# Hybrid GLA and mixture-of-experts layer on one core: routing and collection of expert 0's rows in two steps, its down weights rounded behind the sort

## The chip, the core and the metric

The kernel runs on one core of a Trainium2 chip. The metric is the device time of one execution in microseconds. The engines are TensorE (PE, with its weight loads PEld), VectorE (DVE), ScalarE (ACT), GpSimd (POOL) and SyncE (SP), which issues most of the transfers to the DMA engines.

## The reference

One layer over 512 tokens of width 1024: a gated linear attention mixer, then a grouped top-2 mixture of 16 experts of inner width 512, then a norm. What matters here is the second half:

```python
x = x + g1 * y                                     # y: the mixer's output projection
h2 = _modulate(_rmsnorm(x, norm2_g[i]), sh2, sc2).reshape(n_lat, D_MODEL)
f = _moe(h2, w_router, b_router, w_gate_e[i], w_up_e[i], w_down_e[i])
x = x + g2 * f.reshape(bsz, t, D_MODEL)

def _moe(h, w_router, b_router, w1, w3, w2):
    scores = jax.nn.sigmoid((h @ w_router).astype(jnp.float32))
    sel = scores + b_router.astype(jnp.float32)
    grp = sel.reshape(n, N_EXPERT_GROUPS, EXPERTS_PER_GROUP)
    grp_score = jnp.sum(lax.top_k(grp, TOP_K)[0], axis=-1)
    best = jnp.argmax(grp_score, axis=-1)
    ...
    for e in range(N_EXPERTS):
        he = jax.nn.silu(h @ w1[e]) * (h @ w3[e])
        out = out + gates[:, e:e + 1] * (he @ w2[e])
```

Each token goes to two experts of one group of four. The kernel computes an expert only on the rows that are routed to it.

## The kernel before

**Tiles.** The 512 tokens are four tiles of 128 rows. Products in float32 are made of three matmuls of a faster format: each operand is split into a rounded part (a cast on ScalarE, line 56 or 281) and the rest (a subtraction on VectorE, line 57 or 282). For a chunk of weights this is `conv`; the names `wh`, `wl` and `fx` in the rows are its buffers. One chunk of 128 x 1024 costs one cast and one subtraction.

**Up to the routing.** `project` multiplies a tile by the output weights (lines 51 to 53), `second` makes the tile's second half of the new x (multiply line 717, add line 718, sum of squares on ScalarE line 719), which stays in `srg`. `turn` transposes x on TensorE (725) and copies it out of PSUM (727), `logits` multiplies it by the router weights (732), `score` transposes the result (854) and `add_bias` scales it by the norm (857). The norm itself is `ln_exp` (one VectorE operation at 824, logarithm and exponential on ScalarE at 825 and 826) and `refine` (three VectorE operations, 830 to 832). `scaled` (839) and `normed` (842, with the store to `h2d` in memory at 843) make the normalised and modulated rows, from which the later experts gather.

**Routing.** The sigmoid (904 to 907) gives `sel`. Sixteen VectorE operations (924 to 941) find the best group and its two experts and write the one-hot `ohs` for all four tiles at once; meanwhile `warm` (912) lets TensorE run 11 and later 2 matmuls whose results nobody reads. Eight matmuls of `ohs` with a triangle and with ones (943 to 947) give every token's position in its expert's list and every expert's count; `zm` (951) is the position, masked.

**Experts 0 and 1** are static: their weights are loaded early. Expert 0's rows aren't gathered but collected: `hot` (956) is the one-hot of its positions times the norm, and 32 float32 matmuls (964) of x with it give the collected, transposed rows, which ScalarE modulates (967). Its up projection takes 16 matmuls on unsplit float32 weights (1181; in the trace each float32 matmul of 964 and 1181 leaves two records), its gate product is at 1147 and 1148 (`he`), transposes at 1154, and the down projection uses `conv` on the chunks held in `su2` and `su3`.

**The other experts.** `index_of` makes the list of rows of an expert: a one-hot `ohx` (991), matmuls (997) and two small operations (999, 1018), after which GpSimd gathers the rows from `h2d` (1102). For experts 0 and 1 it is called first. Experts 2 to 15 are sorted by their counts in nine small VectorE operations (1042 to 1052), whose result `eid` gives the number of the expert. SyncE reads these numbers into registers (1305) and issues loads of 1 MB from the addresses that they give (688). Such loads go into buffers of the list `free` as these come free, with at most three outstanding. The first two go into the two halves of `srg`, tiles 0 and 1 and tiles 2 and 3, once nobody needs x there any more:

```python
free = su[4:9] + su[1:4] + [None, None, B[1], su[0]] + [srgf[:, 0:2048], srgf[:, 2048:4096]]
```

**Order.** Up to the collection each engine's instructions are issued in the order in which the code is written. Behind it a scheduler orders them by readiness and priority; `tc.issue_after(x)` puts what stands under it behind the instruction x. On each engine the order is then fixed in the program. Before, `index_of` for the static experts stands behind the last collecting matmul and the sort behind `hot`:

```python
with tc.issue_after(collected[1][1].ins):
    last, rest = index_of(0, tiles[0:NS], lambda e: zm[:, :, e], vals, two=True)
...
for n in (2, 3):
    with tc.issue_after(eidl.ins):
        scaled(n, V, 0, 1)
        normed(n)
```

Of the kernel before, what the change touches and what calls it, by code (L numbers as in the profile page):

```python
# [13 lines left out]
AF = mybir.ActivationFunctionType  # L14
OP = mybir.AluOpType
# [3 lines left out]
P = 128  # L19
# [13 lines left out]
def dit_kernel(ctx: ExitStack, tc: tile.TileContext, I, out):  # L33
# [865 lines left out]
    S.copy(lgT[:, 384:512], plg3)  # L899
    refine(3)  # L900
    score(3)
    for n in range(4):
# [20 lines left out]
    f_, e_ = sg4.unsqueeze(2).to_broadcast([P, 16, 4, 4]), sg4.unsqueeze(3).to_broadcast([P, 16, 4, 4])
    V.tensor_tensor(mx, pr[:, :, 0], pr[:, :, 1], op=OP.max)
    V.tensor_tensor(mn, pr[:, :, 0], pr[:, :, 1], op=OP.add)
    V.tensor_tensor(cb, f_, e_, op=OP.is_equal)
    V.tensor_add(m1, mx[:, :, 0], mx[:, :, 1])
    V.tensor_tensor(m2_, mn[:, :, 0], mn[:, :, 1], op=OP.max)
    V.tensor_tensor(cg, f_, e_, op=OP.is_gt)
    V.tensor_tensor(m1, m1, m2_, op=OP.max)  # L930
    V.tensor_mul(cb, cb, t44.unsqueeze(1).to_broadcast([P, 16, 4, 4]))
    V.tensor_reduce(gm, gs, axis=AX.X, op=OP.max)
    V.tensor_add(cg, cg, cb)
    V.tensor_tensor(gr, gs, gm.unsqueeze(2).to_broadcast([P, 4, 4]), op=OP.is_equal)
    V.tensor_reduce(rk16, cg, axis=AX.X, op=OP.add)
    V.tensor_mul(gr, gr, dn4.unsqueeze(1).to_broadcast([P, 4, 4]))
    V.tensor_reduce(gm, gr, axis=AX.X, op=OP.max)
# [6 lines left out]
    for t in range(3):  # L944
        PE.matmul(pp[:, t + 1:4], ones, ohs[:, t].unsqueeze(1).to_broadcast([P, 3 - t, NE]), start=False, stop=t == 2)
# [594 lines left out]
```

## Time and profile before

| | before |
|---|---|
| time, median of 3 runs | 656.12 us (654.6 to 658.16) |
| profiled execution, time | 656.5 us |
| profiled execution, span | 654.7 us |
| mean granted TensorE clock | 0.975 of full speed |
| busy: PE / DVE / ACT / POOL | 599.0 / 463.6 / 302.6 / 98.3 us |
| moved by DMA | 168.41 MB, mean 257 GB/s |

The span is what the profile covers of the execution, 1.8 us less than its time. Shares of busy time are means over stages with different limits. The change lies between 330 and 375 us of the span, and the views of that stretch are the timeline of each engine (start, duration, what it works on, and in brackets the idle time before it with what ended it), the list of waits, and the table of stretches.

### The profile page before, as it was taken

How to read it: one execution, taken by the hardware profiler on the slowest of the kernel's cores; microseconds unless marked ns; L12 is line 12 of the kernel's file. 1: busy time of each engine (PE TensorE's matmuls, PEld its weight loads, DVE VectorE, ACT ScalarE, POOL GpSimd, SP SyncE). 2: the span in 40 equal slices, each digit the busy share in tenths (PEclk: the TensorE clock that was granted, in tenths of full speed). 3: DMA queues.
4: the chain of work that ended last, by engine and by line, in shares of the span. 5: the costliest groups of instructions: out<-in, count | busy, mean ns of one | idle time of the engine just before them, and what ended most of it. 6: DMA issues, size and time to landing. Idle time of an engine off the chain costs nothing. (4 is left out here: it accounts for less than half of the span.)

```text
span 654.7 us, 11203 instructions
## 1 busy us (share of the span) xinstructions
PE 599.0 (91%) x4200; PEld 412.4 (63%) x4200; DVE 463.6 (71%) x984; ACT 302.6 (46%) x511; POOL 98.3 (15%) x102
## 2 busy tenths in 40 slices
PE   3999999999999999999979989999999999999741
PEld 2778577776878878778748465545565657664310
DVE  5667499849985972575288399465767689999615
ACT  6433399257352233642451255334444457773131
POOL 4030000010100010012200330120322222222032
PEclk9999999999999999999998999999999999999975
DMA  8996472220234861658662989899999999999974
GB/s 269 340 353 218 175 274 66 67 66 4 67 130 158 270 232 51 254 183 354 237 227 74 373 316 366 326 342 351 412 387 395 362 352 358 393 383 345 298 273 189
DMA packets 50251, 168.41 MB, mean 257 GB/s; under 512 B 6779, under 2 KB 17237, under 8 KB 37138
## 3 DMA queue, kind: packets, MB, share of 16 engines
q1 hardware_dynamic: 43216, 156.26, 64.4%
q0 software_dynamic: 5024, 8.70, 5.6%
q10 hardware_dynamic: 1954, 2.71, 1.3%
q8 instruction: 34, 0.56, 0.3%
q14 instruction: 23, 0.19, 0.1%
HBM read 158.64 MB, written 12.30 MB: 261 GB/s over the span
## 5 line engine op out<-in xcount | busy, mean ns | idle before, releaser
L51 PE MATMUL bk<-wh,fh 128*128 128x512 f32 (+3 forms) x276 | 110.9, 409 | 0.7 <-ACT fh L56 0.4
L52 PE MATMUL bk<-wl,fh 128*128 128x512 f32 (+3 forms) x276 | 111.3, 405 | 0.0
L53 PE MATMUL bk<-wh,fl 128*128 128x512 f32 (+3 forms) x276 | 109.0, 399 | 0.5 <-DVE fl L57 0.5
L282 DVE TENSOR_TENSOR wl<-st,wh 128x512 fp32r<-128x512 f32 x60 | 39.9, 685 | 38.9 <-ACT wh L281 37.6
L56 ACT CAST wh<-su 128x1024 fp32r<-128x1024 f32 x45 | 46.8, 1047 | 39.9 <-PE bk L53 38.7
L281 ACT CAST wh<-st 128x512 fp32r<-128x512 f32 x60 | 35.9, 620 | 59.5 <-PE bk L53 50.8
L51 PEld LDWEIGHTS bk<-wh,fh 128*128 128x128 f32 (+3 forms) x276 | 50.2, 183 | 19.2 <-ACT wh L56 3.3
L57 DVE TENSOR_TENSOR wl<-su,wh 128x1024 fp32r<-128x1024 f32 x45 | 54.5, 1222 | 10.5 <-ACT wh L56 8.3
L1106 POOL DMA_INDIRECT accd<-y,gix x16 | 37.2, 2324 | 164.8 <-DVE y L1166 78.2
L52 PEld LDWEIGHTS bk<-wl,fh 128*128 128x128 f32 (+3 forms) x276 | 50.6, 183 | 16.5 <-issue 3.3
L53 PEld LDWEIGHTS bk<-wh,fl 128*128 128x128 f32 (+3 forms) x276 | 50.6, 183 | 13.7 <-issue 1.2
L1202 PE MATMUL bk<-su,he 128*64 128x512 f32 (+1 forms) x136 | 21.7, 526 | 12.5 <-DMA su<-in_w_down_e_dram 9.6
L1202 PE MATMUL bk<-su,xg 128*32 128x256 f32 (+1 forms) x216 | 31.7, 485 | 1.5 <-DVE xg L1196 1.5
L56 ACT CAST fx<-su 128x1024 fp32r<-128x1024 f32 x21 | 22.0, 1050 | 21.8 <-PE bk L53 21.6
L57 DVE TENSOR_TENSOR fx<-su,fx 128x1024 fp32r<-128x1024 f32 x21 | 25.7, 1222 | 7.4 <-ACT fx L56 7.2
L51 PE MATMUL bk<-fx,fh 128*128 128x512 f32 (+3 forms) x68 | 27.9, 410 | 1.2 <-ACT fh L56 1.2
L52 PE MATMUL bk<-fx,fh 128*128 128x512 f32 (+3 forms) x68 | 27.3, 402 | 1.0 <-DVE fx L57 1.0
L53 PE MATMUL bk<-fx,fl 128*128 128x512 f32 (+3 forms) x68 | 26.6, 394 | 0.2 <-DVE fl L57 0.2
L1102 POOL DMA_INDIRECT xg<-h2d,gix x16 | 20.1, 1259 | 39.2 <-DVE pis L1005 15.1
L250 POOL DMA_DIRECT2D mrd<-mrow x8 | 3.8, 487 | 129.2 <-DVE mrow L248 129.2
L1202 PEld LDWEIGHTS bk<-su,he 128*64 128x64 f32 (+1 forms) x136 | 6.6, 127 | 24.4 <-DMA su<-in_w_down_e_dram 11.0
L57 DVE TENSOR_TENSOR fl<-bk,fh 128x512 fp32r<-128x512 f32 (+3 forms) x25 | 15.5, 634 | 7.5 <-ACT fh L56 5.5
(476 smaller groups left out, 1303.6 us busy)
## 6 DMA issues: line engine op xcount, KB each, us to landing
su<-in_w_up_e_dram SPq DMA_DIRECT2D x23, 1024.0 KB, 8.2
su<-in_w_down_e_dram SPq DMA_DIRECT2D x21, 1024.0 KB, 7.8
su<-in_w_gate_e_dram SPq DMA_DIRECT2D x19, 1024.0 KB, 8.3
st<-in_gla_w_in_dram SPq DMA_DIRECT2D x10, 1024.0 KB, 5.0
QQ<-in_w_mod_dram SPq DMA_DIRECT2D x5, 1024.0 KB, 10.8
st<-in_w_gate_e_dram SPq DMA_DIRECT2D x5, 1024.0 KB, 6.8
st<-in_w_up_e_dram SPq DMA_DIRECT2D x5, 1024.0 KB, 9.0
B<-in_w_mod_dram SPq DMA_DIRECT2D x4, 1024.0 KB, 5.1
```

The costliest lines, as they stand in the source:

```text
L51: PE.matmul(o, ah, bh, start=first, stop=False)
L52: PE.matmul(o, ah, bl, start=False, stop=False)
L53: return PE.matmul(o, al, bh, start=False, stop=last)
L56: S.copy(hi, full)
L57: return V.tensor_sub(lo, full, hi.bitcast(F32))
L250: G.dma_start(mrd[4 * h_ + c4:4 * h_ + c4 + 1, :], mrow[32 * c4:32 * c4 + 1, :])
L281: S.copy(w[0][:, k], st[:, k])
L282: mark[0] = V.tensor_sub(w[1][:, k], st[:, k], w[0][:, k].bitcast(F32))
L1102: G.indirect_dma_start(out=xg, out_offset=None, in_=src, in_offset=bass.IndirectOffsetOnAxis(ap=idx, axis=0), bounds_check=n - 1, oob_is_e ...
L1106: G.indirect_dma_start(out=dst, out_offset=bass.IndirectOffsetOnAxis(ap=idx, axis=0), in_=y, in_offset=None, bounds_check=n - 1, oob_is_er ...
L1202: PE.matmul(o[s.w * a:s.w * a + s.w], l, r(a), start=first, stop=last, tile_position=(0, s.w * a))
```

## The change

The lines below are those of the kernel after; its lines are up to 29 higher than before.

- `scaled(1)` and `normed(1)` leave the stretch ahead of the routing and stand behind the sort, as tiles 2 and 3 did. `turn(2, 1)` and `ln_exp(2)` change places with `project(3, 6, 7)`. `turn(3, 1)` is copied by ScalarE instead of VectorE.
- Sigmoid and the sixteen operations are made for tiles 0 to 2 and again for tile 3 (`gated`, `routed`), the positions and one-hots too (`placed`). The collection's matmuls are 24 for tiles 0 to 2 and 8 for tile 3 (`collect`), into two PSUM banks that two matmuls of one row prime ahead. The eight position matmuls with the counts stand between the 24 and the 8. `warm` is called once, with 5.
- The sort is still behind the last `hot`, which now is tile 3's. `index_of` of experts 0 and 1 is behind the sort.
- The subtractions (line 57) for expert 0's down weights that were issued early (three of four) are behind the sort; the casts stay where they were.

```diff
     turn(0, 1)
     second(2)
-    scaled(1, V, 1)
-    normed(1)
     project(3, 4, 5)
-    ln_exp(2)
     turn(1, 1)
     logits(0, 1)
+    turn(2, 1)
     project(3, 6, 7)
+    ln_exp(2)
     refine(2)
     logits(1, 1)
-    turn(2, 1)
     second(3)
...
-    turn(3, 1, V)
     logits(2, 1)
-    ln_exp(3)
     V.tensor_copy(lgT[:, 0:384], plg[:, 0:3].rearrange("p n t -> p (n t)"))
-    logits(3, 1)
     for n in range(3):
         score(n)
...
+    turn(3, 1)
+    ln_exp(3)
+    for n in range(3):
         add_bias(n)
-    scored = [S.activation(sc, lg, AF.Exp, scale=-1.0)]
-    V.tensor_scalar(sc, sc, 1.0, None, op0=OP.add)
-    V.reciprocal(sc, sc)
-    V.tensor_add(sel, sc, brb.unsqueeze(1).to_broadcast([P, 4, NE]))
...
-    warm(11)
...
+    def placed(a, b):
+        V.scalar_tensor_tensor(zm[:, a:b], pp[:, a:b], 1.0, ohs[:, a:b], op0=OP.add, op1=OP.mult)
+        for t in range(a, b):
+            hotl = V.tensor_scalar(hot[:, t], iot[:, 0:P], zm[:, t, 0:1], rstd2[:, t:t + 1], op0=OP.is_equal, op1=OP.mult)
+        return hotl
+
+    def collect(ts):
+        for k4 in range(2):
+            for k in range(4):
+                kt = 4 * k4 + k
+                for t in ts:
+                    m = PE.matmul(pts[k4][:, k], x1[:, t, kt * P:(kt + 1) * P], hot[:, t], start=False, stop=t == 3 and k == 3)
+        return m
+
+    gated(0, 3)
+    logits(3, 1)
+    S.copy(lgT[:, 384:512], plg3)
+    refine(3)
+    score(3)
+    pts = []
+    for k4 in range(2):
+        pts.append(bank())
+        PE.matmul(pts[k4], xgb[0][0:1, 0:P], xgb[0][0:1, 0:512], start=True, stop=False)
...
+    warm(5)
+    routed(0, 3)
+    add_bias(3)
...
+    gated(3, 4)
+    placed(0, 3)
+    collect(range(3))
+    routed(3, 4)
+    for o, ts in ((3, (3, 0, 1, 2)), (4, range(4))):
+        for i, t in enumerate(ts):
+            PE.matmul(pp[:, o], tri if o == 3 and i == 0 else ones, ohs[:, t], start=i == 0, stop=i == 3)
+    hotl = placed(3, 4)
+    m = collect([3])
...
-    with tc.issue_after(collected[1][1].ins):
-        last, rest = index_of(0, tiles[0:NS], lambda e: zm[:, :, e], vals, two=True)
...
-    for n in (2, 3):
+    with tc.issue_after(collected[1][1].ins), tc.issue_after(eidl.ins):
+        _, rest = index_of(0, tiles[0:NS], lambda e: zm[:, :, e], vals, two=True)
+    for n in (1, 2, 3):
         with tc.issue_after(eidl.ins):
-            scaled(n, V, 0, 1)
+            scaled(n, V, *range(n == 1, 2))
             normed(n)
...
                 if not s.raw:
-                    ws = conv(w.rearrange("p (a n) -> p a n", a=2))
+                    with ExitStack() as cc:
+                        if s is ex[0]:
+                            cc.enter_context(tc.issue_after(eidl.ins))
+                        ws = conv(w.rearrange("p (a n) -> p a n", a=2))
```

VectorE's order from the sort's last instruction on, before (`eid` is the list of sorted experts; `h_3360` is tile 2, the `xg` of line 839 is tile 3, `oh` and `zk` belong to the gates and ranks of the sorted experts):

```order
L1052 CAST eid<-eidf 128x14
L839 TENSOR_TENSOR h_3360<-srg,xg 128x512 x2
L839 TENSOR_TENSOR xg<-srg,xg 128x512
L842 SCALAR_TENSOR_TENSOR h_3360<-h_3360,rstd_2742,xg 128x1024
L999 SCALAR_TENSOR_TENSOR ixf<-bk,pid 128x2
L839 TENSOR_TENSOR xg<-srg,xg 128x512
L1018 TENSOR_TENSOR gix<-bk,ixf 128x2
L842 SCALAR_TENSOR_TENSOR xg<-xg,rstd_2742 128x1024
L1065 SCALAR_TENSOR_TENSOR oh<-rk_3234,gr 128x64 x2
L1067 SCALAR_TENSOR_TENSOR zk<-oh,zm 128x56
```

The same place after (`h_3024` is tile 1):

```order
L1076 CAST eid<-eidf 128x14
L1018 TENSOR_TENSOR ohx<-iot,zm 128x512 x2
L839 TENSOR_TENSOR h_3024<-srg,xg 128x512
L1026 SCALAR_TENSOR_TENSOR ixf<-bk,pid 128x2
L842 SCALAR_TENSOR_TENSOR h_3024<-h_3024,rstd_2742,xg 128x1024
L1045 TENSOR_TENSOR gix<-bk,ixf 128x2
L839 TENSOR_TENSOR xg<-srg,xg 128x512 x2
L1091 SCALAR_TENSOR_TENSOR oh<-rk_3205,gr 128x64
L842 SCALAR_TENSOR_TENSOR xg<-xg,rstd_2742 128x1024
L1091 SCALAR_TENSOR_TENSOR oh<-rk_3205,gr 128x64
L57 TENSOR_TENSOR fx<-su_2694,fx 128x1024
```

The two index one-hots and tile 1 now stand ahead of tile 3, tile 2 is no longer among these rows, and the first subtraction of the down weights has come in.

VectorE's order up to expert 0's gate product `he`, before (`zk`, `rv`, `zp` are the ranks of the sorted experts):

```order
L1071 TENSOR_TENSOR big_3268<-zk,perm 128x784
L1084 RECIPROCAL wsum<-wsum 128x4
L1072 TENSOR_REDUCE zk<-big_3268 128x56
L1073 TENSOR_SCALAR rv<-zk 128x4x14
L1074 SCALAR_TENSOR_TENSOR zp<-rv,zk 128x56
L991 TENSOR_TENSOR ohx<-iot_2993,zp 128x512
L1148 TENSOR_TENSOR he<-he,bk 128x512
```

After, from the reciprocal on (`h_3377` is tile 2):

```order
L1110 RECIPROCAL wsum<-wsum 128x4
L57 TENSOR_TENSOR wl_486<-su_2694,wh_485 128x1024
L839 TENSOR_TENSOR h_3377<-srg,xg 128x512 x2
L1097 TENSOR_TENSOR big_3254<-zk,perm 128x784
L842 SCALAR_TENSOR_TENSOR h_3377<-h_3377,rstd_2742,xg 128x1024
L1098 TENSOR_REDUCE zk<-big_3254 128x56
L57 TENSOR_TENSOR wl_488<-su_2695,wh_487 128x1024
L1099 TENSOR_SCALAR rv<-zk 128x4x14
L1100 SCALAR_TENSOR_TENSOR zp<-rv,zk 128x56
L1018 TENSOR_TENSOR ohx<-iot_2993,zp 128x512
L1174 TENSOR_TENSOR he<-he,bk 128x512
```

Two more subtractions and tile 2 now stand ahead of the gate product.

SyncE's order around the first loads of sorted experts, before (`h2d` are the stores of the normalised tiles):

```order
L1305 TENSOR_LOAD eid
L1305 ISA x2
L688 ISA
L688 DMA srg<-in_w_gate_e_dram 128x2048
L843 DMA h2d<-h_3360 128x1024
L843 DMA h2d<-xg 128x1024
L688 ISA
L688 DMA srg<-in_w_up_e_dram 128x2048
L688 ISA
L688 DMA su_2696<-in_w_gate_e_dram 128x2048
```

After:

```order
L688 DMA srg<-in_w_gate_e_dram 128x2048
L843 DMA h2d<-h_3024 128x1024
L843 DMA h2d<-xg 128x1024
L1334 TENSOR_LOAD eid
L1334 ISA x2
```

```order
L1334 TENSOR_LOAD eid
L1334 ISA x2
L688 ISA
L688 DMA srg<-in_w_up_e_dram 128x2048
L843 DMA h2d<-h_3377 128x1024
L688 ISA
L688 DMA su_2696<-in_w_gate_e_dram 128x2048
```

Three register reads stand ahead of the first load instead of four; between the two pieces after are two further reads, so that four stand ahead of the second load, and tile 2's store is behind it.

## Rows read from the trace of the kernel before

**Rows 1.** Page, busy time by engine: us (share of the span) xinstructions.

```profile
PE 599.0 (91%) x4200; PEld 412.4 (63%) x4200; DVE 463.6 (71%) x984; ACT 302.6 (46%) x511; POOL 98.3 (15%) x102
```

**Rows 2.** Waits of PE, 372 to 605 us: us in total, times, longest us.

```profile
PE bk L1154 <- DVE he L1148: 2.1, 4, 0.8
...
PE bk L51 <- ACT wh L56: 0.2, 1, 0.2
```

**Rows 3.** Waits of PE, 605 us to the end.

```profile
PE bk L1202 <- DMA su<-in_w_down_e_dram: 9.6, 2, 8.9
```

**Rows 4.** Stretches: length, busy us of each engine, then granted clock, DMA share, GB/s.

```profile
342.40:349.30 6.90, 6.77 (x27) 5.38 (x27) 5.34 (x28) 0.53 (x2) 0.00 (x0) 0.51 0.59 213
...
384.00:388.00 4.00, 3.03 (x12) 1.91 (x12) 4.00 (x17) 2.00 (x2) 2.34 (x3) 1.00 0.29 99
...
400.00:452.00 52.00, 51.52 (x292) 26.05 (x290) 33.73 (x70) 19.70 (x24) 8.24 (x6) 1.00 0.92 344
452.00:600.00 148.00, 144.98 (x689) 90.78 (x686) 121.51 (x212) 84.83 (x99) 36.72 (x19) 1.00 1.01 377
```

**Rows 5.** Waits of the queue that SP issues to, 384 to 460 us.

```profile
SPq L688 <- PE bk L1202: 30.2, 9, 6.5
```

**Rows 6.** Timeline of DVE, 333 to 341 us: start, us, what [idle before <-releaser].

```profile
333.57 0.68 DVE L839 TENSOR_TENSOR h<-srg,xg 128x512 f32<-128x512 f32 x1
334.36 1.29 DVE L842 SCALAR_TENSOR_TENSOR h<-h,rstd,xg 128x1024 f32<-128x1024 f32 x1
...
339.16 1.22 DVE L57 TENSOR_TENSOR wl<-su,wh 128x1024 fp32r<-128x1024 f32 x1
340.29 0.69 DVE L718 TENSOR_TENSOR srg<-srg,su 128x512 f32<-128x512 f32 x1
```

**Rows 7.** Timeline of PE, 341 to 381 us.

```profile
341.12 0.63 PE L725 MATMUL bk<-ident,srg 128*128 128x128 f32 x4 [3.72 <-DVE srg L718]
...
344.85 4.81 PE L912 MATMUL bk<-fh 128*128 128x512 f32 x11
...
350.76 7.51 PE L964 MATMUL bk<-hot,srg 128*128 128x128 f32 x64
...
358.31 13.98 PE L1181 MATMUL bk<-su,full 128*128 128x512 f32 x32
...
380.45 1.07 PE L1136 MATMUL bk<-ident,xg 128*128 128x128 f32 x8
```

**Rows 8.** Timeline of ACT, the cast of a down-weight chunk.

```profile
336.26 1.05 ACT L56 CAST fx<-su 128x1024 fp32r<-128x1024 f32 x1
```

**Rows 9.** Timeline of DVE, 351 to 373 us.

```profile
351.39 1.29 DVE L991 TENSOR_TENSOR ohx<-iot,zm 128x512 bf16<-128x512 bf16 x2
352.61 0.36 DVE L1042 TENSOR_TENSOR big<-cnt 128x196 f32<-128x196 f32 x1
...
355.52 0.18 DVE L1052 CAST eid<-eidf 128x14 int32<-128x14 f32 x1
...
363.85 0.18 DVE L1084 RECIPROCAL wsum<-wsum 128x4 f32<-128x4 f32 x1 [1.41 <-POOL wsum L1082]
...
372.40 0.69 DVE L1148 TENSOR_TENSOR he<-he,bk 128x512 f32<-128x512 f32 x1 [6.18 <-PE bk L1181]
```

**Rows 10.** Timeline of SP's issues, 358 to 362 us.

```profile
358.57 0.37 SPq L688 DMA_DIRECT2D srg<-in_w_gate_e_dram  x1
...
360.77 0.33 SPq L843 DMA_DIRECT2D h2d<-xg  x1
361.41 0.50 SPq L688 DMA_DIRECT2D srg<-in_w_up_e_dram  x1
```

**Rows 11.** The first gather: its start, its landing (356 to 384 us), the stores' landing (line 843).

```profile
368.87 1.10 POOL L1102 DMA_INDIRECT xg<-h2d,gix  x1 [2.59 <-DMA h2d<-xg]
...
xg<-h2d,gix POOLq DMA_INDIRECT x1, 6.8
...
DMA to landing us min/median/max: 2.7/5.3/7.9
```

More of the change, by code (lines that the diff above doesn't have):

```diff
@@ L891, in dit_kernel, with gated @@
     pf = [bank()[:, 0:4 * NE].rearrange("p (n e) -> p n e", n=4) for _ in range(2)]
-    turn(3, 1, V)
     logits(2, 1)
-    ln_exp(3)
     V.tensor_copy(lgT[:, 0:384], plg[:, 0:3].rearrange("p n t -> p (n t)"))
-    logits(3, 1)
     for n in range(3):
         score(n)
[L899 to L902, printed above, removed]
+    turn(3, 1)
+    ln_exp(3)
+    for n in range(3):
         add_bias(n)
-    scored = [S.activation(sc, lg, AF.Exp, scale=-1.0)]
-    V.tensor_scalar(sc, sc, 1.0, None, op0=OP.add)
-    V.reciprocal(sc, sc)
-    V.tensor_add(sel, sc, brb.unsqueeze(1).to_broadcast([P, 4, NE]))
+    scored = []
+    def gated(a, b):
+        ts = slice(a, b)
+        scored.append(S.activation(sc[:, ts], lg[:, ts], AF.Exp, scale=-1.0))
+        V.tensor_scalar(sc[:, ts], sc[:, ts], 1.0, None, op0=OP.add)
+        V.reciprocal(sc[:, ts], sc[:, ts])
+        V.tensor_add(sel[:, ts], sc[:, ts], brb.unsqueeze(1).to_broadcast([P, b - a, NE]))
     def warm(n):
@@ L922, in dit_kernel @@
     cg = big2[:, 128:256].bitcast(BF16).rearrange("p (t e f) -> p t e f", t=16, e=4)
[L923 to L937, printed above, removed]
-    V.tensor_tensor(gr, gr, gm.unsqueeze(2).to_broadcast([P, 4, 4]), op=OP.is_equal)
@@ L939, in dit_kernel @@
     grb = gr.rearrange("p t g -> p (t g)").unsqueeze(2).to_broadcast([P, 16, 4])
     ohs = R("ohs", [4, NE], BF16)
-    V.scalar_tensor_tensor(ohs.rearrange("p t (g e) -> p (t g) e", g=4), rk16, 1.5, grb, op0=OP.is_lt, op1=OP.mult)
-    pp = bank(pb)[:, 0:5 * NE].rearrange("p (t e) -> p t e", t=5)
-    PE.matmul(pp[:, 0:4], tri, ohs, start=True, stop=False)
-    for t in range(3):
-        PE.matmul(pp[:, t + 1:4], ones, ohs[:, t].unsqueeze(1).to_broadcast([P, 3 - t, NE]), start=False, stop=t == 2)
@@ new lines, in dit_kernel @@
+    gated(0, 3)
[7 more added lines that the diff above has]
+        PE.matmul(pts[k4], xgb[0][0:1, 0:P], xgb[0][0:1, 0:512], start=True, stop=False)
+    pts = [p_.rearrange("p (k t) -> p k t", k=4) for p_ in pts]
+    warm(5)
+    routed(0, 3)
+    add_bias(3)
+    pp = bank(pb)[:, 0:5 * NE].rearrange("p (t e) -> p t e", t=5)
+    PE.matmul(pp[:, 0:3], tri, ohs[:, 0:3], start=True, stop=False)
@@ L953, in dit_kernel @@
+    for t in range(2):
+        PE.matmul(pp[:, t + 1:3], ones, ohs[:, t].unsqueeze(1).to_broadcast([P, 2 - t, NE]), start=False, stop=t == 1)
     hot = mo.tile([P, DE], F32, tag="he", name="hot", bufs=3).rearrange("p (t s) -> p t s", t=4)
     big1 = mo.tile([P, D], F32, tag="t4", name="big1", bufs=NY)
-    for t in range(4):
-        hotl = V.tensor_scalar(hot[:, t], iot[:, 0:P], zm[:, t, 0:1], rstd2[:, t:t + 1], op0=OP.is_equal, op1=OP.mult)
-    def collect(k4):
-        pt = bank().rearrange("p (k t) -> p k t", k=4)
+    gated(3, 4)
@@ L960, in collect @@
+    placed(0, 3)
[6 more added lines that the diff above has]
+    m = collect([3])
+    collected = []
+    for k4 in range(2):
         full = mo.tile([P, DE], F32, tag="he", name="full", bufs=3).rearrange("p (k t) -> p k t", k=4)
@@ L962, in collect @@
             kt = 4 * k4 + k
-            for t in range(4):
-                m = PE.matmul(pt[:, k], x1[:, t, kt * P:(kt + 1) * P], hot[:, t], start=t == 0, stop=t == 3)
-        for k in range(4):
-            kt = 4 * k4 + k
-            S.activation(full[:, k], pt[:, k], AF.Identity, scale=m2T[:, 8 + kt:9 + kt], bias=m2T[:, kt:kt + 1])
-        return full, m
-    collected = [collect(k4) for k4 in range(2)]
+            S.activation(full[:, k], pts[k4][:, k], AF.Identity, scale=m2T[:, 8 + kt:9 + kt], bias=m2T[:, kt:kt + 1])
+        collected.append((full, m))
+    scored = scored[1:]
     ctx2.close()
```

34 lines of the change are left out of this document (26 added, 8 removed).

## Prediction

> **What bounds the kernel now.** I read the busy times first, then the list of what TensorE waits for, then the stretch that the change touches on each engine's timeline. TensorE is busy for 91% of the span [rows 1]. From 372 us (the end of expert 0's up projection) to 605 us the list of its waits has six rows, all on VectorE or ScalarE and 7 us in sum; the first and the last are shown [rows 2]. Only behind 605 us does it wait for weights [rows 3]. So between 372 and 605 us nothing but TensorE's own order gives time back: what TensorE is late by at 372 us, it is late by at 605 us.
>
> The DMA engines are nearly idle in 384 to 388 us (share 0.29) and not full in 400 to 452 us (0.92), and full from 452 us on (1.01) [rows 4]. In the two stretches that aren't full the queue that issues the weight loads waits 30.2 us for TensorE's reading of the buffers [rows 5]. Loads therefore start when TensorE has freed a buffer, and a late TensorE makes the full stretch behind 452 us late by as much. That carries a delay over to the end, where weights are waited for [rows 3].
>
> **Up to the collection (gain).** VectorE's tile 1 multiply (0.68) and normalisation (1.29) and the three subtractions of expert 0's down weights (1.22 each) lie ahead of tile 3's last residual add, which starts at 340.29 [rows 6]; TensorE waits 3.72 us for it [rows 7]. All five leave this place. The add doesn't come earlier by their sum: the refining of tile 2's norm needs ScalarE's exponential, which now stands behind the rounding of a down-weight chunk that starts at 336.26, when the projection has used its buffer (1.05) [rows 8]. So 336.3 + 0.3 (it now stands behind one more copy) + 1.05 + 0.2 for the exponential gives 337.8, 0.6 for the refining 338.4, and 0.7 for the multiply ahead of the add 339.1: 1.2 us earlier.
>
> From there tiles 0 to 2 go alone: scores at 340.3, tile 3's copy on ScalarE ahead of their exponential until 342.5, the gate's three operations until 343.7, tile 3's refining 0.6, the sixteen operations 2.6 (2.96 with four tiles), then tile 3's gate until 348.0, and the first one-hot. The collection starts at 348.6 instead of 350.76 [rows 7]. Its 32 matmuls take 7.51 us, 0.235 each [rows 7]; 24 take 5.6, and some 0.5 more while the clock is still low, to 354.6. Tile 3's own sixteen operations lie under these 24 (they end at 351) and cost nothing. But its eight position matmuls stand behind the 24 in TensorE's order: product 0.25, one-hot 0.4, together a wait of 0.9, then 8 x 0.235. The collection ends at 357.4 instead of 358.3. Of 2.1 us gained at its start 0.9 is left at its end. The two priming matmuls and the shorter fill (5 instead of 11 + 2) stand where TensorE waits for VectorE, and cost nothing.
>
> **The sort and the index (loss).** The counts come out of the last position matmuls, and the sort follows the last one-hot. It starts at 355.5 instead of 352.61 [rows 9]: the expert list is ready at 358.5, not 355.5, **3.0 us later**. The two index one-hots (1.29 together) were ahead of the sort and hidden under the collection [rows 9]; now they are behind it, 358.5 to 359.8, and TensorE waits 1.9 us between collection and index. Expert 0's first matmul starts at 359.4, not 358.31 [rows 7]: 1.1 us later. Its 13.98 us on TensorE don't change, so they end 1.1 later too.
>
> **VectorE's queue behind the sort (loss, on the path).** Everything that left the early place comes back here: two index one-hots 1.29, tile 1's multiply and normalisation 0.68 + 1.29, three subtractions 3.66, together 6.9, or 6.4 when each starts 0.1 before its predecessor's end, as 339.16 + 1.22 against 340.29 shows [rows 6]. They all stand ahead of expert 0's gate product. That product waits 6.18 us for TensorE today [rows 9]: this is the cover of the whole edit. It comes 3.0 + 6.4 = 9.4 later by VectorE, so the cover is used up and 3.2 is left. The 1.41 wait for GpSimd's sums [rows 9] is part of today's queue; moved work that falls into it shortens this, to 1.8 at best. One subtraction stands just ahead of that wait; I take **2.8** (between 1.8 and 3.2). The product's input from TensorE is only 1.1 later, so VectorE is what comes last. Transposes and down projection of expert 0 wait behind it.
>
> **The gather of expert 1's rows.** It needs all four normalised tiles in memory. The last store leaves at 360.77 today and the gather starts at 368.87, 2.59 of this as a wait [rows 10, 11]. Now the last is tile 2's: on VectorE 13.3 us of queue stand from the list's end to the end of its normalisation (index one-hots 1.2, tile 1 1.8, two subtractions 2.3, tiles 3 and 2 4.9, the rank product and small ones 1.8, the wait for GpSimd 1.3), so it leaves at 371.9. On the issuing queue the first weight load goes out 2.9 later than today, with the list; the store also stands behind four register reads and the second weight load, which waits for tile 2's multiply and goes out at 369.8 instead of 361.41 [rows 10]. A store lands 5.3 us later at the median, 2.7 at the least, 8.1 for today's last one (360.77 to 368.87) [rows 10, 11]: 377.2. The gather lands 6.8 us behind its start [rows 11]: 384.0 (381.4 to 386.8). TensorE transposes these rows at 380.45 today [rows 7], at 383.3 with the 2.8: another **0.7** (0 to 3.5). The store goes out just behind a 1 MB load on one queue. The Trainium skill (DMA: Bandwidth & Descriptors, "Queues, rings and completion order") says that each DMA engine takes up a ring's descriptors in order; by it the least landing time is out of reach here and the wait is nearer to 1 than to 0, and the sum would be some 0.3 higher.
>
> The loads themselves: eight are late by up to 8.4 us at first, but the idle 384 to 388 us lies behind them, and the next buffer (expert 1's) comes free only when VectorE has read it, 3.5 late. Loads have caught up with TensorE by then.
>
> **Sum.** 2.8 + 0.7 = 3.5 us late at about 386 us, kept to the end. The profiled execution took 656.5 us (span 654.7 and 1.8 around it): 660.0. The median of the runs is 0.4 lower: **659.6**.
>
> **Rivals.**
> (a) Lag carried through, as above: 2.5 to 4.8, so 658.6 to 661; 0.54.
> (b) TensorE's clock. The row of 342.4 to 349.3 us shows a granted clock of 0.51 [rows 4], the level of 1.2 GHz, behind the 3.72 us of waiting; it came back to 2.4 GHz while TensorE ran the eleven fill matmuls without a gap [rows 7]. Now five stand there and a wait of 0.9 precedes the collection. If the clock comes back only in the midst of the 24 matmuls, 12 of them cost 0.235 more: 2.8, and all behind moves, 662.4 (all 24: 665). For it: less fill and more gaps. Against it: the two priming matmuls fill too, and the first wait is shorter. Low clock in expert 0's up projection alone would cost nothing up to the 1.7 us by which VectorE is later there. In the Trainium skill (TensorE: Matmul & The Clock Gate, Part 1, "What's actually happening") the low clock is the default and activity releases it; by this rule taking fill away can only prolong the low stretch, which is this case. 0.20.
> (c) Not slower: the delay is absorbed behind 400 us. The place is 400 to 452 us, where the DMA engines have 8% of 52 us, 4.2 us, to spare [rows 4]. If loads there were started ahead of need rather than by TensorE's release, they would catch up, the full stretch would start on time, and the wait of 9.6 us behind 605 us [rows 3] would swallow what TensorE is late by: 656.5 to 657. It decides at 452 us: loads on time there, or 3.5 late. Against it stand the 30.2 us of waiting for TensorE [rows 5]. 0.17.
> (d) Faster: the early part gains much more than 2.1 us, because ScalarE's rounding doesn't hold the refining and the shorter wait keeps the clock at 2.4 GHz. VectorE's product then needs the list by 355.5 + 6.18 + 1.4 - 6.4 = 356.7 to be no later than today; that is 1.8 earlier than I find, and the 24 matmuls alone forbid it unless the collection starts at 346.8. Beyond that point expert 0 starts earlier by what is left, 1 to 4 us: 653 to 655. 0.09.
>
> **Chances.** 0.5% of the time, 3.3 us, is about what a measurement of this kernel can tell from no change. Slower by more (over 659.4): half of (a), 0.28, and (b), 0.20: 0.48. Within: the rest of (a), 0.26, (c), 0.17, and part of (d): 0.45. Faster: 0.07. The range leaves out most of (d), a little of (c) and the far end of (b): 656.0 to 663.0.
>
> **What would show it.** Right: the collection starts near 348.6 and ends near 357.4; the list at 358.5; TensorE idle some 1.9 ahead of the index and some 2.5 ahead of expert 0's transposes, released by VectorE's product near 375.2; the last store at 372 and a gather near 377; the first loads into expert 1's buffers 3 to 4 us later. Wrong: a product that still waits for TensorE (the queue is cheaper than I count), transposes of expert 1 that wait over 2 us for the gather, a granted clock of 0.5 behind 350 us, or a release of buffers in 400 to 452 us that isn't late.

## The result, and the profile after

The kernel after takes **666.93 us** (median of four runs, 665.51 to 668.36), the kernel before 656.05: a ratio of **1.0161 [1.0139, 1.0184]**. It is slower, as forecast, but by 10.9 us and not by 3.5, and the time lies outside the range. The profiled execution took 668.1 us (span 666.3).

The page of the kernel after, busy time by engine, answers to [rows 1]:

```profile
PE 606.4 (91%) x4199; PEld 416.6 (63%) x4199; DVE 465.3 (70%) x1003; ACT 302.7 (45%) x513; POOL 101.3 (15%) x102
```

TensorE has one record fewer (eight fill matmuls less, four priming records and three position matmuls more), yet it is busy 7.4 us longer. That is a first sign of its clock. The stretches of the kernel after, answering to [rows 4] (length, busy us of PE, PEld, DVE, ACT and POOL, then granted clock, DMA share, GB/s), show where it was low:

```profile
336.00:339.80 3.80, 1.43 (x20) 0.75 (x18) 1.86 (x6) 2.59 (x5) 0.00 (x0) 0.99 0.00 0
339.80:356.40 16.60, 14.31 (x52) 9.97 (x53) 8.61 (x52) 2.32 (x8) 0.00 (x0) 0.50 0.37 128
356.40:380.80 24.40, 20.02 (x94) 11.62 (x92) 18.66 (x38) 5.53 (x12) 6.79 (x12) 0.99 0.43 144
380.80:387.50 6.70, 5.46 (x14) 4.18 (x15) 1.51 (x3) 1.63 (x2) 1.10 (x1) 0.50 1.02 426
...
400.00:452.00 52.00, 51.03 (x279) 27.37 (x278) 36.99 (x84) 22.73 (x28) 10.02 (x7) 1.00 0.92 347
452.00:600.00 148.00, 145.50 (x708) 91.11 (x708) 118.37 (x191) 84.01 (x97) 35.56 (x18) 1.00 1.00 374
```

A granted clock of 0.50 is 1.2 of 2.4 GHz. It stood for 16.6 us through routing and collection, where the kernel before had 6.9 us of it [rows 4], and again for 6.7 us at the turn from expert 0 to expert 1, where the kernel before has 1.00:

```profile
370.00:380.00 10.00, 8.48 (x34) 5.59 (x32) 3.83 (x4) 4.33 (x5) 0.00 (x0) 1.00 1.01 420
```

TensorE's timeline in the kernel after, answering to [rows 7], says what stood there (start, us, what, idle time before and its releaser):

```profile
340.35 1.46 PE L854 MATMUL bk<-sel,he 128*128 128x16 f32 x6 [2.92 <-DVE he L891]
...
345.00 3.78 PE L970 MATMUL bk<-xg 1*128 1x512 f32 x4
...
348.70 2.50 PE L910 MATMUL bk<-fh 128*128 128x512 f32 x5
...
352.00 7.90 PE L959 MATMUL bk<-hot,srg 128*128 128x128 f32 x48 [0.68 <-DVE hot L951]
...
364.45 1.10 PE L1207 MATMUL bk<-su,full 128*128 128x512 f32 x2
...
381.36 1.11 PE L1180 MATMUL bk<-ident,he 128*128 128x128 f32 x4 [2.74 <-DVE he L1174]
...
391.11 1.07 PE L1162 MATMUL bk<-ident,xg 128*128 128x128 f32 x8
```

Line 970 holds the two priming matmuls (four records, as the 24 of the collection are 48); they contract one row. With the fill behind them they keep TensorE from 345.00 to 351.20. The collection starts at 352.00, not at 350.76 as before, and its 24 matmuls take 7.90 us, more than the 32 of before took (7.51) [rows 7]. VectorE's timeline shows who waits for whom:

```profile
339.13 0.69 DVE L718 TENSOR_TENSOR srg<-srg,su 128x512 f32<-128x512 f32 x1
...
347.77 0.21 DVE L945 SCALAR_TENSOR_TENSOR ohs<-rk,gr 128x48 bf16<-128x48 f32 x1
...
351.35 0.21 DVE L949 SCALAR_TENSOR_TENSOR zm<-bk,ohs 128x48 f32<-128x48 f32 x1 [2.27 <-PE bk L978]
...
363.51 0.17 DVE L1076 CAST eid<-eidf 128x14 int32<-128x14 f32 x1
...
380.63 0.68 DVE L1174 TENSOR_TENSOR he<-he,bk 128x512 f32<-128x512 f32 x1
```

Tile 3's residual add came 1.2 us earlier than before [rows 6], just as forecast. The one-hots of tiles 0 to 2 were ready at 347.98. The positions that VectorE needs next come from TensorE behind priming and fill, so VectorE waited 2.27 us. The list of sorted experts stands at 363.51, the gate product at 380.63.

From expert 1 on the lateness stays what it is. Two products of VectorE far apart, in the kernel before:

```profile
396.57 0.69 DVE L1148 TENSOR_TENSOR he<-he,bk 128x512 f32<-128x512 f32 x1
...
584.66 1.40 DVE L1166 SCALAR_TENSOR_TENSOR y<-bk,gsl,g1b 88x512 f32<-88x512 f32 x2
```

and in the kernel after:

```profile
407.25 0.69 DVE L1174 TENSOR_TENSOR he<-he,bk 128x512 f32<-128x512 f32 x1
...
595.37 1.40 DVE L1192 SCALAR_TENSOR_TENSOR y<-bk,gsl,g1b 88x512 f32<-88x512 f32 x2
```

They are 10.68 and 10.71 us late. TensorE's wait behind 615 us answers to [rows 3] and hardly grew, so nothing was taken back there:

```profile
PE bk L1228 <- DMA su<-in_w_down_e_dram: 10.1, 2, 9.9
```

The store that the gather waits for, tile 2's, leaves at 377.51 and lands 4.5 us later; the gather starts at 382.98 (first row; the second is its time to landing):

```profile
382.98 1.10 POOL L1128 DMA_INDIRECT xg<-h2d,gix  x1 [5.18 <-DMA h2d<-h]
...
xg<-h2d,gix POOLq DMA_INDIRECT x1, 7.7
```

It lands 7.7 us later, at 390.7, just ahead of the transposes at 391.11. It is not what came last.

### The profile page after: what moved, and what is told of

The parts are those of the page before. It is cut to its first block, busy times and chain, and to the rows that moved or that the text cites. A ratio compares the mean times of both kernels' runs of the same rounds, so it can differ in the third digit from the quotient of the medians.

```text
span 666.3 us, 11217 instructions
## 1 busy us (share of the span) xinstructions
PE 606.4 (91%) x4199; PEld 416.6 (63%) x4199; DVE 465.3 (70%) x1003; ACT 302.7 (45%) x513; POOL 101.3 (15%) x102
## 5 line engine op out<-in xcount | busy, mean ns | idle before, releaser
L1228 PE MATMUL bk<-su,he 128*64 128x512 f32 (+1 forms) x136 | 21.7, 526 | 12.5 <-DMA su<-in_w_down_e_dram 10.1
L1128 POOL DMA_INDIRECT xg<-h2d,gix x16 | 19.9, 1245 | 36.7 <-DVE pis L1032 11.6
```

The source lines that it names most:

```text
L1128: G.indirect_dma_start(out=xg, out_offset=None, in_=src, in_offset=bass.IndirectOffsetOnAxis(ap=idx, axis=0), bounds_check=n - 1, oob_is_e ...
L1228: PE.matmul(o[s.w * a:s.w * a + s.w], l, r(a), start=first, stop=last, tile_position=(0, s.w * a))
```

## The experiments

All are compared with runs of the kernel before on the same chip, by ratios; 0.0010 is 0.66 us. The median of before was 655.86 us beside e1 to e4, 658.28 beside e5 to e8 and 657.27 beside e9 to e12, so times of different groups compare by their ratios only. "Lag" is how late the profiled execution is against the profile of before from about 400 us on; it is 10.7 for the kernel after. Part of a lag can be older than the edit. VectorE's multiply (line 717) that starts at 306.35 us both before and after lies ahead of all that the edits move. There e2, e3 and e4 are already late by 0.95, 1.21 and 0.93 us, e5 by 3.03, e7, e9, e10 and e12 by 0.4 to 0.7; e1 is early by 0.35 and e6 by 0.66; e8 and e11 are within 0.1.

**Is it the clock, and which part of it? Runs e1_fill_gap and e2_wide_prime.** The first puts fill into TensorE's wait of 2.92 us at 337.4, the second lets the priming matmuls contract 128 rows of zeros. The edits to the kernel after (of the first, the lines that take the bank `pf` whole for the fill are not shown):

```diff
...
     logits(2, 1)
+    for _ in range(12):
+        PE.matmul(pf[1], hhl[0][:, 0:P], hhl[0], start=True, stop=True)
...
```

```diff
-        PE.matmul(pts[k4], xgb[0][0:1, 0:P], xgb[0][0:1, 0:512], start=True, stop=False)
+        PE.matmul(pts[k4], xgb[0][:, 0:P], xgb[0][:, 0:512], start=True, stop=False)
```

> The changed kernel with twelve fill matmuls (128x512, nobody reads them) ahead of the first score, where TensorE waits 2.9 us for tile 3. Clock theory: the low clock from 339.9 to 356.4 us begins because of that wait; with the fill the granted clock stays at 1.00, the priming and fill matmuls behind it take 3.0 instead of 6.3 us, the collection starts at about 349 instead of 352, its first 24 matmuls take 5.6 instead of 7.9, the list of experts is ready at about 358.6 instead of 363.6, and the time falls by 5 us or a little more, to 661 to 662. Rival (the clock falls all the same at a later wait, or the delay isn't carried to the end): 665 or more.

> The changed kernel with the two priming matmuls contracting 128 rows of zeros instead of one row; the same columns, the same time on TensorE at one clock. Theory: matmuls of one row do not help to bring the clock back, those of 128 rows do; then the clock returns before the collection (by about 350 us instead of 356.4), the 24 matmuls take 5.6 instead of 7.9 us, and the time falls by 2.3 to 3 us, to 664. Rival (rows make no difference, only the five fill matmuls do): clock back at 356.4 as before, 667.

With the gap filled: 665.57 us, 1.0151 [1.0103, 1.0200], not told apart from the change itself: a miss, 661 to 662 was expected. Its stretches show why:

```profile
336.00:345.90 9.90, 8.84 (x59) 5.54 (x58) 6.29 (x29) 4.36 (x11) 0.00 (x0) 1.00 0.60 199
345.90:353.20 7.30, 6.06 (x31) 5.45 (x30) 4.09 (x28) 0.22 (x1) 0.00 (x0) 0.54 0.05 20
353.20:386.50 33.30, 26.10 (x129) 16.11 (x128) 24.45 (x47) 10.33 (x17) 7.90 (x13) 1.00 0.62 227
386.50:393.00 6.50, 5.11 (x22) 3.94 (x23) 3.05 (x17) 1.17 (x2) 0.00 (x0) 0.52 0.90 378
```

and its TensorE timeline:

```profile
343.14 1.98 PE L973 MATMUL bk<-xg 1*128 1x512 f32 x4
...
348.23 7.74 PE L962 MATMUL bk<-hot,srg 128*128 128x128 f32 x48 [1.24 <-DVE hot L954]
...
377.44 0.66 PE L1183 MATMUL bk<-ident,he 128*128 128x128 f32 x4 [2.74 <-DVE he L1177]
...
384.47 0.36 PE L1044 MATMUL bk<-rv,ohx 128*128 128x7 bf16 x8
...
387.89 1.97 PE L1165 MATMUL bk<-ident,xg 128*128 128x128 f32 x8 [2.96 <-DMA xg<-h2d,gix]
```

The wait no longer lowers the clock, the collection starts at 348.23 (forecast 348.6). But the clock falls at 345.9, under the fill that follows the one-row matmuls, though TensorE had had no wait over 0.7 us since 337 us; the 24 matmuls still take 7.74. The wait of 2.74 us ahead of expert 0's transposes (line 1183) is the same as in the kernel after, but here the clock stays at 1.00 through it: a wait of this length need not bring the low clock. From VectorE's product (376.70) to line 1044 it takes 7.77 us, against 10.16 for the same instructions in the kernel after (380.63 to 390.79, line 1041 there), where the clock fell: that is what the second low stretch costs, 2.4 us. Being earlier by 4, the kernel then waits 2.96 for the gather, and the clock falls there. Lag 8.0.

With priming over 128 rows: 664.60 us, 1.0134 [1.0110, 1.0158]. The time is the expected one, but its interval overlaps that of the change, so the reading rests on the trace. The stretches:

```profile
340.60:351.10 10.50, 8.74 (x29) 5.43 (x29) 5.91 (x32) 2.32 (x8) 0.00 (x0) 0.51 0.58 201
351.10:362.00 10.90, 8.32 (x77) 7.77 (x75) 6.55 (x34) 2.10 (x7) 0.00 (x0) 1.00 0.01 2
```

The same matmuls at the same length (3.76 us at line 970) now bring the clock back at 351.1 and not at 356.4, and the 24 take 5.69 us. Rows are all that differs, so one-row priming is what left the clock low. The other runs bear it out: the three other profiled kernels with one-row priming behind an unfilled wait were low for some 17 us (e3, e5) and 13.6 (e4), against 10.5 here; and the mean granted clock is 0.969 or 0.970 in all runs of e2, 0.962 to 0.968 in the four of the change. Lag 7.7.

**Both together: e8_fill_wide.** The edit is that of both runs.

> The changed kernel with both: twelve fill matmuls in the wait ahead of the first score and priming matmuls of 128 rows. Theory: the clock stays at 1.00 from 336 us to the end of the collection, the 24 matmuls take 5.6 instead of 7.7, so the list of experts is 2.1 earlier than with the fill alone (357.5), the gate product at 374.6. The gather of expert 1's rows stays what comes last (3 us of waiting, low clock behind it); TensorE is 6 us later than in the kernel before at 400 us instead of 8.0: 662 to 664. If the last weights set the end, up to 2 more. Rival (the gather doesn't follow the list): TensorE 3 us later than before at 400 us, 659.6.

662.53 us, **1.0070 [1.0042, 1.0097]**: clear of the change, of e1 and of e2, and the forecast's ratio (659.6 / 656.12 = 1.0053) lies within. Its stretches:

```profile
342.90:346.30 3.40, 3.16 (x6) 1.61 (x7) 3.23 (x20) 0.19 (x1) 0.00 (x0) 0.54 0.92 346
376.20:380.90 4.70, 4.02 (x13) 3.07 (x14) 0.69 (x1) 1.09 (x2) 1.10 (x1) 0.64 1.01 425
```

its TensorE timeline:

```profile
348.95 5.69 PE L962 MATMUL bk<-hot,srg 128*128 128x128 f32 x48 [0.68 <-DVE hot L954]
...
376.10 0.65 PE L1183 MATMUL bk<-ident,he 128*128 128x128 f32 x4 [2.74 <-DVE he L1177]
...
385.50 1.09 PE L1165 MATMUL bk<-ident,xg 128*128 128x128 f32 x8 [0.44 <-DMA xg<-h2d,gix]
```

and its VectorE:

```profile
358.26 0.17 DVE L1079 CAST eid<-eidf 128x14 int32<-128x14 f32 x1
...
375.37 0.68 DVE L1177 TENSOR_TENSOR he<-he,bk 128x512 f32<-128x512 f32 x1
```

Collection, list and product now stand where the forecast has them (348.6, 358.5, 375.2). The low stretch in front is 3.4 us instead of 16.6, not gone as I had expected: the clock falls at about 343, ahead of the priming (which starts at 343.58), so a fall here needs no one-row matmuls. The second low stretch remains, 4.7 us long. Expert 1's transposes are 5.1 us late, and from 400 us the lag is 4.5. The time lies in the expected 662 to 664, but not by the steps that I gave for it: the gather was to be last by 3 us and is by 0.44, and the lag was to be 6.

**Which part of the change pays? e3_subs_early** (the change with the subtractions where they were) and **e4_index_early** (the change with the lists of experts 0 and 1 where they were). The first against the kernel after:

```diff
-                    with ExitStack() as cc:
-                        if s is ex[0]:
-                            cc.enter_context(tc.issue_after(eidl.ins))
-                        ws = conv(w.rearrange("p (a n) -> p a n", a=2))
+                    ws = conv(w.rearrange("p (a n) -> p a n", a=2))
```

> The changed kernel with the three subtractions of expert 0's down weights back where they were before the change (ahead of tile 3's multiply). Queue theory: VectorE's queue behind the sort sets expert 0's gate product; without the subtractions it is 3.4 us shorter, TensorE's wait of 2.74 us ahead of the transposes falls to under 1, the second stretch of low clock (380.9 to 387.5) goes with it (2.4 us), and the front costs up to 1 us; 667 minus 4 to 5, so 662 to 663. Rival (the queue isn't what counts, only the late collection): within 1 us of 667.

671.28 us, 1.0243 [1.0211, 1.0275]: a miss. I had put what the subtractions cost ahead of the sort at 1 us at most, and left out the gather. TensorE's timeline:

```profile
343.60 1.46 PE L854 MATMUL bk<-sel,he 128*128 128x16 f32 x6 [4.96 <-DVE he L891]
...
382.56 0.66 PE L1180 MATMUL bk<-ident,he 128*128 128x128 f32 x4 [1.02 <-DVE he L1174]
...
395.12 1.97 PE L1162 MATMUL bk<-ident,xg 128*128 128x128 f32 x8 [5.10 <-DMA xg<-h2d,gix]
```

The wait ahead of expert 0's transposes fell to 1.02, about as expected, and the clock stayed up there. But the residual add of tile 3 slid to 342.39 and the first wait grew from 2.92 to 4.96; the collection came 3.2 us later, of which this execution was late by 1.2 already. The store of tile 2 left at 379.29, the gather started 6.95 behind it and was then last by 5.10. So in the change the late subtractions are a gain.

The second edit:

```diff
     vals = lambda e: rv[:, :, e]
+    with tc.issue_after(collected[1][1].ins):
+        _, rest = index_of(0, tiles[0:NS], lambda e: zm[:, :, e], vals, two=True)
...
-    with tc.issue_after(collected[1][1].ins), tc.issue_after(eidl.ins):
-        _, rest = index_of(0, tiles[0:NS], lambda e: zm[:, :, e], vals, two=True)
```

> The changed kernel with the row lists of experts 0 and 1 ahead of the sort again. TensorE's wait of 1.56 us ahead of the index goes, expert 0's up projection starts 1.5 us earlier, the list of experts is 1.2 later. Queue theory: the gate product is set by VectorE's queue, which is as long as it was, so the time stays within 0.7 us of 667 (TensorE waits longer ahead of the transposes instead). Rival (the start of expert 0 counts): 1.5 us less, 665.4.

669.57 us, 1.0197 [1.0175, 1.0220]: 2.6 us more than the 667 expected, though the interval overlaps that of the change. TensorE's row ahead of expert 0's transposes:

```profile
380.66 1.11 PE L1180 MATMUL bk<-ident,he 128*128 128x128 f32 x4 [4.25 <-DVE he L1174]
```

Expert 0 starts earlier (362.43 beside 364.45) and then waits longer for VectorE's product (4.25 beside 2.74), as expected. The lag at 400 us is 10.1; it grows to 13.6 between 577 and 627 us, where instructions stand in another order. Why is not settled, so the run doesn't show what the place of the lists costs in time.

**The parts by themselves, on the kernel before.** Run e5_two_steps_alone is the kernel after with tile 1, the exponential's and copy's order, the subtractions and the lists put back (the edits of the last two runs, `for n in (2, 3)` and the old order in front); e6_subs_late_alone, e9_index_late_alone and e10_tile1_late_alone make one move each on the kernel before. The edit of e6 is the reverse of that of e3; the other two:

```diff
-    with tc.issue_after(collected[1][1].ins):
-        last, rest = index_of(0, tiles[0:NS], lambda e: zm[:, :, e], vals, two=True)
...
+    with tc.issue_after(collected[1][1].ins), tc.issue_after(eidl.ins):
+        _, rest = index_of(0, tiles[0:NS], lambda e: zm[:, :, e], vals, two=True)
```

```diff
-    scaled(1, V, 1)
-    normed(1)
...
-    for n in (2, 3):
+    for n in (1, 2, 3):
         with tc.issue_after(eidl.ins):
-            scaled(n, V, 0, 1)
+            scaled(n, V, *range(n == 1, 2))
```

> The routing and collection in two steps alone: as in the changed kernel, but tile 1's normalisation, the norm of tile 2, the subtractions and the row lists of experts 0 and 1 stand where they stood before. Theory: the two steps themselves make the list of experts late (the counts wait for the 24 matmuls, and the low clock stretches them), by 5 to 7 us against the kernel before, but VectorE's queue behind the sort is as short as before, so only what is over the cover of 6.2 us and the late start of expert 0 (3 to 5 us) come through: 659 to 661. Rival (the two steps are the whole loss): 666 or more. Second rival (two steps cost nothing, the moved work does): 656 to 657.

> The kernel before with one part of the change alone: the three subtractions of expert 0's down weights behind the sort. Queue theory: VectorE's queue behind the sort grows by 3.4 us, under the cover of 6.2 us in which the gate product waits for TensorE, and tile 3's last add no longer has subtractions ahead of it, so it starts up to 3 us earlier, TensorE's wait of 3.7 us ahead of tile 3's transposes shrinks to about 1, the low clock of 342 to 349 us may not come at all, and all behind is 3 to 4 us earlier: 652 to 653. Rival (subtractions behind the sort are on the path, as in the changed kernel): 656 to 659.

> The kernel before with the row lists of experts 0 and 1 behind the sort, and nothing else. Theory: with one collection of 32 matmuls the sort lies under it, list at 354.3, one-hots until 355.6, the collection until 358.3, so TensorE doesn't wait for the lists and the time is that of the kernel before within 0.5 us. Rival (the order of lists and sort costs as in the changed kernel, where TensorE waits 1.6 us): 1.2 to 1.6 us slower.

> The kernel before with tile 1's multiply and normalisation behind the sort, and nothing else. Theory: the subtractions and their casts, not tile 1, set when tile 3's last add starts, so the front gains 0.5 us at most; the last store leaves at about 367 instead of 360.8, the gather lands at about 379, before TensorE wants it at 380.5: the time is that of the kernel before within 0.7 us. Rival (the later store makes the gather the last): 1 to 3 us slower.

Two steps alone: 664.63 us, **1.0094 [1.0061, 1.0128]**. That is more than the 659 to 661 expected (1.005 to 1.008), but the interval reaches into it. Its profiled execution took 671.72, 5.7 above any other of its runs, and was 3.0 us late at 306 us, so the time is used and not the lag. Lists late alone: 657.69, 0.9991 [0.9960, 1.0022]; tile 1 late alone: 657.77, 1.0011 [0.9977, 1.0045]; neither is told apart from no change, as expected. In the profiled execution of the second (660.17 us, among its slowest) the gather is last by 1.86 us, so its place isn't free there. Subtractions late alone: 653.21, **0.9935 [0.9910, 0.9960]**, faster than both kernels. TensorE's timeline of e6:

```profile
337.40 0.63 PE L725 MATMUL bk<-ident,srg 128*128 128x128 f32 x4 [0.66 <-DVE srg L718]
...
346.41 7.51 PE L964 MATMUL bk<-hot,srg 128*128 128x128 f32 x64
```

its low stretch:

```profile
340.50:344.00 3.50, 3.50 (x9) 2.75 (x9) 3.07 (x17) 0.26 (x1) 0.00 (x0) 0.51 0.97 359
```

and VectorE's gate product:

```profile
368.05 0.69 DVE L1148 TENSOR_TENSOR he<-he,bk 128x512 f32<-128x512 f32 x1 [2.78 <-PE bk L1181]
```

The wait of 3.72 us [rows 7] is 0.66 and the low stretch 3.5 us long instead of 6.9, so the collection starts 4.35 us earlier (0.66 of it older than the edit). The product behind the sort still waits 2.78 us for TensorE (6.18 before [rows 9]): the three subtractions lie under this wait. The lag is -4.3, kept up to 615 us and the size of the gain in time; this execution, the fastest of its seven, gains 1.9 more behind that.

**Is the wait of 3.72 in the kernel before worth anything without the move? e7_before_fill.** Fourteen fill matmuls in that wait (again without the lines for `pf`):

```diff
...
+    for _ in range(14):
+        PE.matmul(pf[1], hhl[0][:, 0:P], hhl[0], start=True, stop=True)
...
     turn(3, 1, V)
```

> The kernel before with fourteen fill matmuls in TensorE's wait of 3.7 us ahead of tile 3's transposes. Clock theory: the clock stays at 2.4 GHz where it was at 1.2 from 342.4 to 349.3 us, the scores take 0.9 instead of 1.9 us, logits and transposes some 0.3 less, the rest of that stretch is VectorE's; all behind is 1 to 1.3 us earlier: 654.6 to 655. Rival (VectorE and ScalarE set that stretch): 656.

657.28 us, 0.9993 [0.9961, 1.0025]: no gain seen; the 1 to 1.3 us expected are too little for this interval to exclude. Its stretches:

```profile
336.00:350.30 14.30, 11.02 (x79) 7.66 (x77) 12.03 (x42) 4.90 (x11) 0.00 (x0) 1.00 0.52 189
350.30:353.50 3.20, 3.06 (x15) 3.00 (x15) 3.17 (x11) 0.00 (x0) 0.00 (x0) 0.51 0.02 5
```

The low stretch moved behind another wait, of 2.27 us ahead of 349.45, and now lies on the collection, whose 32 matmuls take 8.96 us instead of 7.51. The collection starts 0.26 us earlier than before and ends 1.2 later (0.4 of it older than the edit): what is won in front is lost there.

**Everything but the two steps: e11_one_step_rest** (the moves of e6, e9 and e10, and the order of copy and exponential, on the kernel before), and **e12_subs_tile1_late** (e6 and e10).

> The change without its two steps: routing and collection of all four tiles at once as before, with 11 and 2 fill matmuls, and all the moved work as in the changed kernel (tile 1, the norm of tile 2, the subtractions, the lists of experts 0 and 1). Theory: the loss sits in the two steps and in the low clock and late list that come with them; without them the front gains 1.2 us, the list is ready at about 354, the product and the gather are within 1 us of what TensorE wants: 655 to 657. Rival (the moved work itself is the loss): 660 or more.

> The kernel before with the subtractions and tile 1 behind the sort, the norm of tile 2 where it was: the two moves of the change that should gain or cost nothing alone. Theory: as with the subtractions alone (4 us less than before), since tile 3's add already waits for TensorE's last projection there; the gather comes 2 to 3 us later but still in time: 0.6% faster than before, 652. Rival (the later store makes the gather the last): 1 to 2 us worse than the subtractions alone.

e11: 656.10 us, **0.9979 [0.9949, 1.0009]**. All that the change moves on VectorE costs nothing that the runs can tell, without the two steps. But the two steps alone cost 0.94% of the change's 1.61%: e5 and e11 split the change in two, their ratios multiply to 1.0073, and the rest appears only where both come together. The product row of e11:

```profile
371.24 0.69 DVE L1146 TENSOR_TENSOR he<-he,bk 128x512 f32<-128x512 f32 x1 [1.70 <-PE bk L1179]
```

It still waits for TensorE: with the sort in its old place the cover holds.

e12: 658.52 us, 1.0020 [0.9993, 1.0047]: a miss, it loses what e6 gains. TensorE's rows:

```profile
347.67 8.76 PE L962 MATMUL bk<-hot,srg 128*128 128x128 f32 x64
...
382.64 1.97 PE L1134 MATMUL bk<-ident,xg 128*128 128x128 f32 x8 [3.87 <-DMA xg<-h2d,gix]
```

Here the low clock lies on the collection (8.76 us instead of 7.51), and the gather is last. Tile 2's multiply stands behind all three subtractions and behind VectorE's wait for GpSimd's sums, its store leaves at 368.22 and the gather starts at 373.65. In e11 it stands ahead of that wait and of two of the three, the store leaves at 363.49, and the transposes don't wait. So the gather that the prediction reckoned with is real; it decides when tile 2 stands late in VectorE's queue. How much of the loss is the gather's and how much the low clock's isn't separated.

## Why the prediction was right in direction and too small

The steps against the traces (us; e8 is the change with the low stretch in front cut to 3.4 us):

| | before | forecast | after | e8 |
|---|---|---|---|---|
| tile 3's add | 340.29 | 339.1 | 339.13 | 339.12 |
| collection starts | 350.76 | 348.6 | 352.00 | 348.95 |
| its 24 matmuls | | 6.1 | 7.90 | 5.69 |
| list of experts | 355.52 | 358.5 | 363.51 | 358.26 |
| expert 0's first matmul | 358.31 | 359.4 | 364.45 | 359.20 |
| gate product | 372.40 | 375.2 | 380.63 | 375.37 |
| tile 2's store | | 371.9 | 377.51 | 372.25 |
| gather | 368.87 | 377.2 | 382.98 | 377.66 |
| expert 1's transposes | 380.45 | 384.0 | 391.11 | 385.50 |

- **What bounds the kernel: right.** What TensorE is late by at 391 us (10.66), VectorE's product is late by at 595 (10.71), and the weights' wait behind it takes nothing back. Rival (c), absorption, is out: the 52 us from 400 on have a DMA share of 0.92 in the kernel after as before, and the lag doesn't shrink.
- **Front: right in VectorE's part, wrong in TensorE's.** The add, and the order of what follows, came to 0.03 us. The step that failed is "the two priming matmuls and the shorter fill ... stand where TensorE waits for VectorE, and cost nothing". They were priced at full clock. TensorE idled for 2.92 us, the clock fell meanwhile, at 339.8, and at the low clock they last until 351.20, 3.2 us past the one-hots that were ready at 347.98. The clock came back only at 356.4. Cost: 3.4 at the collection's start, 1.8 in the 24 matmuls, 5.0 at the list. e8 shows it by taking most of it away: each step up to the gate product returns to within 0.4 us of the forecast, and the time falls by 0.9% (1.0161 to 1.0070). Filling the wait alone (e1) or the row count alone (e2) did not do it.
- **Rival (b) was this mechanism, under-sized.** Its bounds, 662.4 and 665, priced low clock in the 24 matmuls alone; it left out the matmuls ahead of them and the second place. The Trainium skill (TensorE: Matmul & The Clock Gate, Part 1, "What's actually happening") has the low clock as the default that activity lifts. The direction agrees: with five fill matmuls instead of eleven the low stretch was longer, 16.6 beside 6.9 us. But being busy did not keep it up: in e1 and e8 the clock fell with no wait over 0.7 us since 337 us, and in the kernel after it stayed low through the 3.78 us of one-row matmuls. What made it fall in e1, e6 and e8 is open.
- **Sort and list: right.** 3.0 late was forecast; 2.7 in e8. The kernel after has 5.3 more, from the step above.
- **VectorE's queue behind the sort: right.** 2.8 forecast at the product, 2.97 in e8. That the cover is used up shows in TensorE's idle 2.74 ahead of line 1180, as forecast (2.5).
- **What that idle does: missed.** I priced it as a delay alone. The clock fell in it, at about 380.8, and from product to expert 1's transposes it took 10.48 us instead of 8.05: 2.4, where I had 0.7 for the gather. In e1 the same idle of 2.74 passed at 1.00, and the stretch behind it had its old length; so the 2.4 is the clock's, and whether the clock falls there varies. That low clock in expert 0's up projection alone would cost nothing was not put to the test (0.99 from 356.4 to 380.8), and it hid that a low stretch behind the product lies on the path.
- **The gather: sized right, not decisive.** Store and gather came to 0.5 us of the forecast in e8. The store landed 4.5 us behind its issue in the kernel after, and the gather started 1.0 later; I had put 5.3 and nothing between, so that the sum fits is in part luck. The least, 2.7, was out of reach. The Trainium skill (DMA: Bandwidth & Descriptors, "Queues, rings and completion order") has that each engine takes up the descriptors of a ring in order. The 4.5 us agree with it, behind a 1 MB load that left 1.9 us earlier, but no run here shows the order itself. In the kernel after it came just in time, in e8 0.44 late, and last by 2.96, 5.10 and 3.87 in e1, e3 and e12.
- **The sum.** 3.5 forecast, 5.4 more at the product and 1.7 more behind it: 10.6, as measured at expert 1's transposes. The 0.9 us left to the profiled execution's 11.6 arise behind 595 us, where the order of rows differs; they weren't followed up.
- **The parts don't add.** The ratios of e5, e6, e9 and e10 multiply to 1.0030, those of e5 and e11 to 1.0073 (by their intervals good to some 0.006 and 0.005); the change has 1.0161. The cover behind the sort holds for each moved part alone (the product still waits for TensorE, by 2.78 us in e6, 6.14 in e9, 4.65 in e10) and, with the sort in its place, for all (1.70 in e11). In the change the sort comes later and the product waits no more. That this, and not the clock alone, makes the rest of the difference is argued from these waits; no run separates the two. Rival (d), faster, needed the list by 356.7; e6 shows that the gain in front is to be had, with the sort untouched.

## What to carry over

Work moved under another engine's wait is free only while what ends that wait stays put: with the subtractions moved alone 0.65% is gained, and in the change, where the sort is later too, the product has no cover left (though there too their late place was the better one, e3). A new wait of TensorE of 3 us is to be priced twice, as delay and as the low clock that may come with it, and matmuls added as filler or priming at the low clock's length too. To beat both kernels, take the three subtractions behind the sort and nothing else (653.21 us, 0.9935 [0.9910, 0.9960]).

## What the runs showed of the hardware

- Matmuls that contract one row did not bring the clock back: in the kernel after four records fill 345.00 to 348.78 and the clock stays at 0.50 until 356.4; with 128 rows of zeros and the same length it is back at 351.1 (e2).
- TensorE's waits that a fall to 1.2 GHz came with or followed: 2.27 us (e7), 2.74 and 2.92 (after), 2.96 (e1), 3.72 (before), 3.87 (e12), 5.10 (e3). A wait of 2.74 in e1 passed without one. It fell with no wait over 0.7 us ahead, too: in e6 at 340.5, 3 us behind a wait of 0.66, under the fill; in e1 at 345.9; in e8 at about 343.
- A low stretch that is filled away can come back later: in e7 it moved by 8 us, and the time stayed (0.9993).
